# A GLA, short-convolution and SwiGLU block on one core: the queues' order is taken from the scheduler's more detailed timeline model

## The chip, the cores and the metric
The kernel runs on one core of a Trainium2 chip. The time is the device time of one execution in microseconds (us), and of several executions the median is taken. A core has five engines, each with its own queue of instructions that it works off in order: TensorE (PE in the profile, with PEld for its weight loads), VectorE (DVE), ScalarE (ACT), GpSimd (POOL) and SyncE (SP, which here only issues DMAs). Engines wait for one another by semaphores.

## The reference
One layer works on 512 latent tokens of width 2048 and 256 context tokens, all in fp32:

```python
hc = modulate(rmsnorm(ctx, norm1_g), sh1c, sc1c)       # context: only k, v and the forget gates are used
o_c, s_f, s_b = gla_bidir(qc, kc, vc, la_fc, la_bc, 0, 0)
hx = modulate(rmsnorm(x, norm1_g), sh1, sc1)
q, k, v, g, lf, lb, cb, cc, cx = split_proj(hx @ w_in)
o_x, _, _ = gla_bidir(q, k, v, la_f, la_b, s_f, s_b)   # 4 heads, forward and backward scan
o   = headwise_rmsnorm(o_x) * gla_g * silu(g)
mix = concat(o, cb * conv_grid(cc * cx, conv_w)) @ w_out
x1  = x + gt1 * mix
h2  = modulate(rmsnorm(x1, norm2_g), sh2, sc2)
out = rmsnorm(x1 + gt2 * ((silu(h2 @ wg) * (h2 @ wu)) @ wd), final_g)
```

The modulation rows (`sh1`, `sc1`, `gt1`, `sh2`, `sc2`, `gt2`) are `silu(c) @ w_mod + b_mod`, and `gla_bidir` is a chunked gated linear attention with data-dependent decay.

## The kernel before
**Products.** Every large product is fp32 made from three fp32r matmuls (`mm3`, L85 to L94): low part of one side by high of the other, high by low, high by high. A weight tile of 128x1024 is loaded by a DMA from SP into `raw` (L118, four buffers) or `ch` (L755, eight), ACT casts it to `whi` (L102), and DVE subtracts to give `wlo` (L103, three buffers each). A unit of the PE's work is the matmuls on one such pair.

**Stages, in the order of time.** (1) From 0 to about 390 us the k and v projections. The normalized input is scaled with modulation columns that the PE makes first from streamed tiles `big<-wsc` (`mod_cols`, L193 to L210, into `pm`); `hhi`, `hlo`, `hhl` and `chl` are its high and low parts. Squares of the input go from ACT to POOL, which adds them (L250). Constants `cid`, `cst` and `gates` are loaded at L265 to L267, and POOL makes eight masks `maskt` from `cst` (L270). (2) From about 390 to 850 us the attention. A function `weave` interleaves one head (`do_gla`) with units of projections (`do_q`, `do_g`, `do_conv`) as filling for the PE. A head has for each direction a chain: ACT makes `qe` and `ke` (L570, L572), DVE multiplies and copies them (L577 to L580; L578 is the last of `qe`) and `kk` (L586), the PE makes scores `psc`, DVE masks them (L596) and adds (L598), then four scan steps follow (`sm` on ACT L610, `pd` and `po` on the PE, `sn` on DVE L618), ACT normalizes (`on`, L633), the PE transposes the result into `pt` (L639) and DVE multiplies it by the gate (L641). Beside that, DVE makes the remaining modulation rows: `mod_some` (L373) multiplies 128 loaded tiles `raw<-wm` of 128x1024 with `cbc` and sums them; each must wait for its load, and its buffer is refilled only when it is done. (3) From about 850 to 1025 us the output projection, as a Strassen-like scheme with seven products (`seven`, steps "1", "5", "63", "7", "24"). The seven left operands are sums and differences of quarters, made by DVE and split into `a0h`, `a0l` to `a6h`, `a6l` (`prep_a`, L701 to L737); the right ones are made in place in `ch` (L782, L788, L793, L807). (4) To about 1125 us the second norm: ACT scales rows (L878), the PE transposes them (L888), ACT modulates (L893), and DVE makes operands again. (5) To about 1950 us the up and gate products of the FFN for eleven column blocks j, each with `seven`; `back` (L957) transposes the activations of the block before, `back_part` splits them and sends them to DRAM. (6) To about 2365 us the down product, and then the final norm (L1087) and the stores.

**What sets the order.** The program text does not fix the order in an engine's queue. The framework's scheduler, which runs when the context `tile.TileContext` closes, takes the instructions with their dependences and writes each engine's queue from a model of when things would be ready. The exception is SP from the start of stage (3) on (L690): there its order is that of the text. Buffers and data dependences are the same in any order.

## Time and profile before

| what | us |
|---|---|
| median of 3 runs (2388.7, 2388.78, 2394.04) | 2388.78 |
| profiled execution | 2393.07 |
| its span in the trace | 2391.3 |
| PE busy | 2252.2 |
| DVE busy | 1704.9 |
| ACT busy | 1030.8 |
| POOL busy | 136.3 |

The profiled execution is thus one of the longer ones, 4.3 us over the median. Its time is 1.8 us more than the span of its instructions. In the views each row has an engine, the line of the kernel, the operation with output and inputs by their names (buffer numbers left out), a count, busy time and, in square brackets or behind a bar, the idle time of that engine just before, with what ended it. PEclk is the granted clock of the PE, 1.00 being full speed; the mean over the execution was 0.973.

### The profile page before, as it was taken

The numbers are of one execution on the slowest core, as the hardware profiler recorded it, in microseconds if no ns is written. First come the engines' busy times: TensorE is split into PE (matmuls) and PEld (weight loads), VectorE is DVE, ScalarE is ACT, GpSimd is POOL, SyncE is SP. The second block draws the span as 40 slices with busy tenths as digits, with TensorE's granted clock in tenths as the row PEclk, the third lists the DMA queues.
The fourth block names the chain that finished last, engine by engine and source line by source line (L and its number), as shares of the span: only waits on it lengthen the run. The fifth ranks groups of instructions, "written<-read, shape, count | busy, mean of one in ns | idle before, by whom it ended". The sixth has DMA issues, their size and how long they took to land.

```text
span 2391.3 us, 27558 instructions
## 1 busy us (share of the span) xinstructions
PE 2252.2 (94%) x10184; PEld 1793.0 (75%) x10184; DVE 1704.9 (71%) x2088; ACT 1030.8 (43%) x1391; POOL 136.3 (6%) x186
## 2 busy tenths in 40 slices
PE   8999999888979969987999999999999999999996
PEld 4765666777868747765888888888888878888875
DVE  3555165665665577768887888788877867787798
ACT  3422055322232344475445554555454544443343
POOL 2422000000000000000000000000000000000001
PEclk9999999999989989998999999999999999999998
DMA  9773466665766244541446434544354494855734
GB/s 326 229 253 111 150 228 194 199 213 187 231 192 217 90 150 128 178 157 52 145 150 203 143 128 145 193 150 142 139 176 159 165 362 151 289 185 178 255 130 141
DMA packets 161619, 431.42 MB, mean 180 GB/s; under 512 B 17867, under 2 KB 38635, under 8 KB 161356
## 3 DMA queue, kind: packets, MB, share of 16 engines
q1 hardware_dynamic: 141612, 380.87, 48.1%
q0 software_dynamic: 8720, 28.58, 3.2%
q10 hardware_dynamic: 11152, 20.21, 2.3%
q8 instruction: 80, 1.31, 0.2%
q14 instruction: 55, 0.45, 0.1%
HBM read 380.82 MB, written 48.78 MB: 180 GB/s over the span
## 4 chain that ended last, share of the span: by engine, by line
issue 57%; POOL 2%; PE 2%; DVE 0%; POOLq 0%; ACT 0%
PE acc L90 2%; POOL opd L971 2%; POOL out L1088 0%; POOL xnd L927 0%; ACT whi L102 0%; DVE xn L925 0%; POOLq L971 0%; DVE wlo L103 0%; DVE u L924 0%; DVE g L922 0%; DVE u L827 0%; POOLq L1205 0%; POOLq L1088 0%; POOLq L927 0%
## 5 line engine op out<-in xcount | busy, mean ns | idle before, releaser
L102 ACT CAST whi<-ch 128x1024 fp32r<-128x1024 f32 x370 | 390.2, 1056 | 461.5 <-PE acc L90 380.4
L103 DVE TENSOR_TENSOR wlo<-ch,whi 128x1024 fp32r<-128x1024 f32 x370 | 450.5, 1224 | 153.8 <-ACT whi L102 153.0
L102 ACT CAST whi<-raw 128x1024 fp32r<-128x1024 f32 x244 | 256.4, 1053 | 405.7 <-PE acc L90 284.9
L103 DVE TENSOR_TENSOR wlo<-raw,whi 128x1024 fp32r<-128x1024 f32 x244 | 302.5, 1240 | 158.8 <-ACT whi L102 158.1
L373 DVE CUSTOM_DVE_ANT_0 raw<-raw,cbc 128x1024 f32<-128x1024 f32 x128 | 156.3, 1224 | 159.6 <-DMA raw<-wm 157.2
L90 PE MATMUL acc<-hhl,whi 128*128 128x512 f32 x640 | 200.0, 393 | 0.0
L90 PE MATMUL acc<-hhi,wlo 128*128 128x512 f32 x320 | 133.4, 418 | 9.1 <-DVE wlo L103 8.3
L90 PEld LDWEIGHTS acc<-hhl,whi 128*128 128x128 f32 x640 | 121.1, 190 | 27.3 <-issue 2.5
L90 PE MATMUL acc<-wlo,a0h 128*128 128x512 f32 x296 | 117.5, 397 | 25.1 <-DVE wlo L103 25.1
L90 PE MATMUL acc<-hhl,wlo 128*128 128x512 f32 x320 | 127.5, 398 | 0.0
L90 PE MATMUL acc<-hlo,whi 128*128 128x512 f32 x320 | 127.2, 397 | 0.2 <-DVE hlo L108 0.2
L90 PE MATMUL acc<-hhi,whi 128*128 128x512 f32 x320 | 126.8, 396 | 0.0
L90 PE MATMUL acc<-whi,a1l 128*128 128x512 f32 x296 | 117.3, 398 | 9.6 <-DVE a1l L103 8.0
L90 PE MATMUL acc<-wlo,a1h 128*128 128x512 f32 x296 | 117.2, 396 | 9.5 <-DVE wlo L103 9.5
L90 PE MATMUL acc<-whi,a6l 128*128 128x512 f32 x296 | 116.4, 395 | 8.8 <-ACT whi L102 7.5
L90 PE MATMUL acc<-whi,a2l 128*128 128x512 f32 x296 | 116.1, 395 | 6.4 <-ACT whi L102 6.4
L90 PE MATMUL acc<-wlo,a2h 128*128 128x512 f32 x296 | 118.0, 399 | 0.9 <-DVE wlo L103 0.9
L90 PE MATMUL acc<-whi,a2h 128*128 128x512 f32 x296 | 117.8, 398 | 0.0
L90 PE MATMUL acc<-wlo,a6h 128*128 128x512 f32 x296 | 116.6, 394 | 0.9 <-DVE wlo L103 0.9
L90 PE MATMUL acc<-whi,a1h 128*128 128x512 f32 x296 | 116.9, 395 | 0.0
L90 PE MATMUL acc<-wlo,a3h 128*128 128x512 f32 x296 | 115.6, 391 | 1.1 <-DVE wlo L103 1.1
L90 PE MATMUL acc<-wlo,a4h 128*128 128x512 f32 x296 | 115.4, 390 | 1.2 <-DVE wlo L103 1.2
(310 smaller groups left out, 4802.8 us busy)
## 6 DMA issues: line engine op xcount, KB each, us to landing
raw<-wm SPq DMA_DIRECT2D x128, 512.0 KB, 4.7
raw<-wu SPq DMA_DIRECT2D x92, 512.0 KB, 4.5
ch<-wu SPq DMA_DIRECT2D x88, 512.0 KB, 3.8
raw<-wc SPq DMA_DIRECT2D x48, 512.0 KB, 3.7
raw<-wd SPq DMA_DIRECT2D x47, 512.0 KB, 6.4
ch<-wd SPq DMA_DIRECT2D x44, 512.0 KB, 6.0
opd<-oh ACTq DMA_DIRECT2D x77, 256.0 KB, 3.1
opd<-ol POOLq DMA_DIRECT2D x77, 256.0 KB, 3.3
```

The source lines that it names most:

```text
L90: nc.tensor.matmul(o, l, r, start=start, stop=stop, skip_group_check=True)
L102: nc.scalar.copy(hi, src)
L103: (eng or nc.vector).tensor_tensor(lo, src, hi, op=ALU.subtract)
L373: nc.vector.tensor_tensor_reduce(out=w, in0=w, in1=cbc[:, hf * 1024 : hf * 1024 + 1024], scale=1.0, scalar=0.0, op0=ALU.mult, op1=ALU.add, ...
L971: nc.gpsimd.dma_start(opd[j][i, 1].rearrange("p k t -> p (k t)"), lo.bitcast(F32))
```

## The change
One argument is added where the kernel opens the context:

```diff
-    with tile.TileContext(nc) as tc:
+    with tile.TileContext(nc, schedule_with_timeline_sim=True) as tc:
         tile_hybrid_block(tc, *args)
```

The scheduler then orders the queues by a more detailed model of the timeline. The instructions are the same on all engines, but for one load of an activation table fewer on ACT. The queues of PE, DVE and ACT are changed in many places, by some rows each; SP and POOL mostly in the first 250 us.

On the PE, in the attention of head 0, the transposes `pt` of the normalized head output `on` stand among the units of a filling projection `acc_3451`. Before:

```order
L90 MATMUL acc_3451<-hhl_539,whi_3454 128x512 x2
L90 MATMUL acc_3451<-hhi_615,wlo_3503 128x512
L639 MATMUL pt_3488<-cidt_70,on_3429 128x128
L639 MATMUL pt_3494<-cidt_70,on_3429 128x128
L90 MATMUL acc_3451<-hlo_616,whi_3502 128x512
L639 MATMUL pt_3488<-cidt_70,on_3429 128x128
L639 MATMUL pt_3494<-cidt_70,on_3429 128x128
```

Now:

```order
L90 MATMUL acc_3451<-hhi_849,whi_3502 128x512
L90 MATMUL acc_3451<-hhl_890,wlo_3503 128x512
L639 MATMUL pt_3488<-cidt_70,on_3429 128x128 x2
L639 MATMUL pt_3494<-cidt_70,on_3429 128x128
L639 MATMUL pt_3488<-cidt_70,on_3429 128x128
L639 MATMUL pt_3494<-cidt_70,on_3429 128x128
```

They stand 15 matmuls of the projection later; in the other heads it is 12 to 18. The second `psc` group (second direction) of head 0 stands 5 matmuls later, that of head 2 seven.

On DVE, in the same stage at head 2, the chain of the two directions (`qe_4527` is the first, `qe_4588` the second) stands among modulation tiles (L373; the second L373 row of each pair reads the sum out). Before:

```order
L578 COPY qe_4527<-big_3249 128x4
L373 ISA raw_4806,modacc_73<-raw_4806,cbc_76 128x1024
L373 ISA modacc_73 128x1
L103 TENSOR_TENSOR wlo_4727<-raw_4724,whi_4726 128x1024
L575 COPY dc_4592<-qe_4588 128x4
L576 TENSOR_TENSOR dc_4592<-qe_4588 128x4
L579 TENSOR_TENSOR ke_4590<-ke_4590,big_1070 128x512
L577 TENSOR_TENSOR qe_4588<-qe_4588,big_3249 128x512
L580 COPY ke_4590<-big_1070 128x4
L586 TENSOR_TENSOR kk_4604<-kk_4604,big_4520 128x512
L578 COPY qe_4588<-big_3249 128x4
L373 ISA raw_4809,modacc_73<-raw_4809,cbc_76 128x1024
```

Now:

```order
L373 ISA raw_4806,modacc_73<-raw_4806,cbc_76 128x1024
L373 ISA modacc_73 128x1
L578 COPY qe_4527<-big_3249 128x4
L373 ISA raw_4809,modacc_73<-raw_4809,cbc_76 128x1024
L373 ISA modacc_73 128x1
L103 TENSOR_TENSOR wlo_4727<-raw_4724,whi_4726 128x1024
L575 COPY dc_4592<-qe_4588 128x4
L576 TENSOR_TENSOR dc_4592<-qe_4588 128x4
L579 TENSOR_TENSOR ke_4590<-ke_4590,big_1070 128x512
L586 TENSOR_TENSOR kk_4604<-kk_4604,big_4520 128x512
L577 TENSOR_TENSOR qe_4588<-qe_4588,big_3249 128x512
L580 COPY ke_4590<-big_1070 128x4
```

Directly behind that come `L373` on `raw_4848` and only then `L578 qe_4588`. One modulation tile has moved ahead of the first direction's last copy, and two more ahead of the second's. In heads 0, 1 and 3 one has moved ahead of the first and one more ahead of the second. The masks and scan steps that follow (L596, L618, L598) also have one or two more ahead of them.

On DVE at the output projection, `wlo_6119` and `wlo_6137` are the low halves of the third and fourth weight pair; the `a` rows are operands of the seven products. Before:

```order
L103 TENSOR_TENSOR a5l_6065<-big_4773,a5h_6064 128x256
L103 TENSOR_TENSOR a6l_6069<-big_4773,a6h_6068 128x256
L103 TENSOR_TENSOR wlo_6119<-ch_6116,whi_6118 128x1024
L103 TENSOR_TENSOR wlo_6137<-ch_6134,whi_6136 128x1024
L103 TENSOR_TENSOR wlo_6160<-ch_6078,whi_6159 128x1024
L782 TENSOR_TENSOR ch_6098<-ch_6177,ch_6098 128x1024
```

Now:

```order
L782 TENSOR_TENSOR ch_6078<-ch_6156,ch_6078 128x1024
L660 TENSOR_TENSOR big_5769<-big_5769,acc_5773 128x512
L782 TENSOR_TENSOR ch_6098<-ch_6177,ch_6098 128x1024
L103 TENSOR_TENSOR wlo_6119<-ch_6116,whi_6118 128x1024
L724 TENSOR_TENSOR s_5888<-big_3014,big_4966 128x256
L724 TENSOR_TENSOR s_5888<-big_3612,big_5187 128x256
```

`wlo_6119` has moved from the end of the operands to ahead of them, some 70 rows. `wlo_6137` follows 19 rows behind it and `wlo_6160` 22 rows behind that, with operand rows between.

Elsewhere: on ACT in stage (4), `whi_7313`, `whi_7332` and `whi_7399` have moved from behind the sixteen-fold L893 to ahead of the first L878; on the PE the transposes L888 now follow the units that use them. On DVE there `wlo_7784` stands 11 rows earlier. On SP a third tile of `wk` and `cid`, `cst` and `gates` (L265 to L267) now come ahead of the second group of `big<-wsc`, and `cbc` (L362) comes in the middle of stage (1); the eight masks L270 are the first work of POOL. In stage (5) the transposes L957 stand 20 to 30 rows earlier on the PE, and on DVE four rows L793 of a block, which read freshly loaded `raw` tiles, stand 3 to 12 rows earlier. At the very end two `wlo` rows of DVE stand 11 or 12 rows earlier.

## Prediction
> **What bounds the kernel now.** I read the page first, then the table of busy time by stage, then what the PE waits for.
>
> ```profile
> span 2391.3 us, 27558 instructions
> PE 2252.2 (94%) x10184; PEld 1793.0 (75%) x10184; DVE 1704.9 (71%) x2088; ACT 1030.8 (43%) x1391; POOL 136.3 (6%) x186
> ```
>
> The PE is idle for 2391.3 - 2252.2 = 139 us. An order can move only that, and the matmuls that ran at a low clock. Next is busy time by stretch: each engine with its count, then the granted clock, the DMA share and GB/s.
>
> ```profile
> 0.00:60.00 60.00, 49.25 (x303) 29.97 (x304) 22.31 (x31) 22.51 (x44) 16.32 (x19) 1.00 1.01 326
> 390.00:850.00 460.00, 417.34 (x1894) 346.36 (x1893) 271.37 (x450) 135.40 (x214) 0.00 (x0) 0.95 0.60 192
> 850.00:900.00 50.00, 24.38 (x98) 18.81 (x96) 43.16 (x95) 26.42 (x63) 0.00 (x0) 0.76 0.34 123
> 1020.00:1125.00 105.00, 81.28 (x351) 65.18 (x352) 83.68 (x111) 71.51 (x117) 2.18 (x4) 0.85 0.32 109
> 1125.00:1890.00 765.00, 764.63 (x3447) 632.95 (x3446) 626.31 (x632) 385.14 (x457) 35.31 (x65) 1.00 0.45 153
> ```
>
> The columns are PE, PEld, DVE, ACT and POOL. The FFN's first stage is full: 764.63 of 765 us, 764.63 / 3447 = 0.222 us a matmul. Idle time lies in four places: attention (460 - 417.34 = 42.7 us), the start of the output projection (25.6), the second norm (23.7) and the first 60 us (10.8). The view of the PE's waits says for whom.
>
> ```profile
> PE acc L90 <- DVE wlo L103: 47.0, 16, 22.2
> PE pt L639 <- ACT on L633: 22.0, 3, 8.7
> PE acc L90 <- ACT whi L102: 15.9, 7, 7.5
> PE psc L90 <- DVE qe L578: 13.5, 4, 3.9
> ```
>
> (Us in total, times, longest.) So a few long waits carry it, in which the PE's queue is stopped by one matmul, while DVE or ACT works off something else that stood ahead.
>
> **The change, part by part.** Each part is held against the profiled execution, 2393.07 us.
>
> *Attention, transposes.* Three transposes `pt` wait 22.0 us together. They now stand some 14 filling matmuls later, 14 x 0.222 = 3.1 us of work for each wait, none of which is as short as that: -9.4 us, if `on` isn't later.
>
> *Attention, chains.* DVE now has modulation tiles ahead of the chain, and these wait for loads. Head 2 in DVE's and SP's timelines:
>
> ```profile
> 659.31 0.17 DVE L578 COPY qe<-big 128x4 f32<-128x4 f32 x1
> 660.12 1.22 DVE L373 CUSTOM_DVE_ANT_0 raw<-raw,cbc 128x1024 f32<-128x1024 f32 x1 [0.65 <-DMA raw<-wm]
> 661.27 1.22 DVE L103 TENSOR_TENSOR wlo<-raw,whi 128x1024 fp32r<-128x1024 f32 x1
> 664.43 0.17 DVE L578 COPY qe<-big 128x4 f32<-128x4 f32 x1
> 664.50 1.22 DVE L373 CUSTOM_DVE_ANT_0 raw<-raw,cbc 128x1024 f32<-128x1024 f32 x1
> 666.98 1.23 DVE L373 CUSTOM_DVE_ANT_0 raw<-raw,cbc 128x1024 f32<-128x1024 f32 x1 [1.25 <-DMA raw<-wm]
> ```
>
> ```profile
> raw<-wm SPq DMA_DIRECT2D x128, 512.0 KB, 4.7
> ```
>
> The page's row gives 4.7 us from issue to landing. The first tile is now ahead of `qe_4527`, whose copy moves from 659.31 to 661.3, behind the wait. The second tile was ready long before 664.50; with it (1.15) and `wlo` (1.15) DVE is at 664.3 when the refill for the third tile can be issued, which in the old order was at 662.5, the end of that `wlo`; it landed there at 666.98, 4.5 later, so now at 668.8. The chain's own four rows take DVE to 666.3, then it stands until 668.8, does the tile (1.15), and copies `qe_4588` at 670.0 instead of 664.43: 5.6 later. The PE does seven matmuls meanwhile (1.6), so 4.0 is lost. The PE waits there already:
>
> ```profile
> 443.30 2.04 PE L90 MATMUL psc<-qe,ke 128*128 128x128 f32 x8 [3.06 <-DVE qe L578]
> ...
> 664.74 2.05 PE L90 MATMUL psc<-qe,ke 128*128 128x128 f32 x8 [3.08 <-DVE qe L578]
> ...
> 783.43 1.13 PE L90 MATMUL psc<-qe,ke 128*128 128x128 f32 x8 [3.25 <-ACT a0h L102]
> ```
>
> Heads 0 and 3 have the same waits at their second `psc`. There one tile is ahead of each direction. In head 0 the second tile landed only after the chain:
>
> ```profile
> 443.96 1.23 DVE L373 CUSTOM_DVE_ANT_0 raw<-raw,cbc 128x1024 f32<-128x1024 f32 x1 [0.81 <-DMA raw<-wm]
> ```
>
> With the chain behind its end at 445.2 (2.1 us, as in head 2 from the end of `wlo` at 662.5 to that of the copy at 664.6) `psc` comes at 447.3: 4.0 later, less five matmuls, 2.9. For head 3, where a tile (1.15) and some operand rows come ahead and nothing fills, I take 3.5; for head 1, without a wait now, 1.5 of the 2.3 that two tiles cost. Sum 4.0 + 2.9 + 3.5 + 1.5 = 11.9, and the attention comes to +2.5 us. Bounds: if those tiles cost nothing, -9.4 and the 2.7 of the filled `psc`, -12; if the scan steps, which also have tiles ahead, deliver `on` later by what the filling gave, +12. I take the middle, since the waits for loads stand in the rows.
>
> *Output projection.* One long wait on the PE, and what DVE did in it:
>
> ```profile
> 857.17 0.73 PE L90 MATMUL acc<-whi,a1l 128*128 128x512 f32 x2 [1.56 <-ACT whi L102]
> 880.07 0.80 PE L90 MATMUL acc<-wlo,a0h 128*128 128x512 f32 x1 [22.17 <-DVE wlo L103]
> 880.66 0.63 PE L90 MATMUL acc<-whi,a0h 128*128 128x512 f32 x1
> 881.09 0.63 PE L90 MATMUL acc<-whi,a0l 128*128 128x512 f32 x1
> ...
> 899.03 0.73 PE L90 MATMUL acc<-whi,a2l 128*128 128x512 f32 x2 [1.67 <-ACT whi L102]
> ```
>
> ```profile
> 857.32 1.10 DVE L726 TENSOR_TENSOR s<-s,big 128x256 f32<-128x256 f32 x3
> ...
> 878.75 3.53 DVE L103 TENSOR_TENSOR wlo<-ch,whi 128x1024 fp32r<-128x1024 f32 x3
> ```
>
> For 878.75 - 857.32 = 21.4 us DVE makes 64 operand rows, 0.335 each, and only then the `wlo`. Now `wlo_6119` comes first, but about 20 rows (6.7 us) stand between it and the next `wlo`, while a unit of 12 matmuls is 2.7 us of PE. The long wait becomes several, each some 4: row by row I get 5.4, 7.0, 3.0, 1.1 and 4.3, 20.8 us, against 1.56 + 22.17 + 1.67 = 25.4. That is -4.6, not -22: DVE was busy 43.16 of 50 us, so at most 6.8 can go without work moved ahead of 850. Bounds -7 and 0.
>
> After such a wait matmuls come 881.09 - 880.66 = 0.43 apart instead of 0.222. [...]
>
> *Second norm.* Two waits:
>
> ```profile
> 1031.22 7.37 ACT L893 ACTIVATE hbig<-pt,modv,gsc 128x256 f32<-128x256 f32 x16
> ```
>
> ```profile
> 1044.94 1.22 PE L90 MATMUL acc<-whi,a6l 128*128 128x512 f32 x2 [7.51 <-ACT whi L102]
> ...
> 1053.46 0.39 PE L90 MATMUL acc<-whi,a0l 128*128 128x512 f32 x1
> ...
> 1106.86 0.80 PE L90 MATMUL acc<-wlo,a1h 128*128 128x512 f32 x1 [8.07 <-DVE wlo L103]
> ```
>
> `whi_7313` stood behind L893 and the casts that follow it, and now comes before; the units run through. But then the PE transposes, and L893 (7.37) with a cast and a split must pass before `a0l`: I count a wait of about 9.6 there, and the matmul of 1053.46 at 1050.6. -3. `wlo_7784` is 11 rows (0.60 each) earlier on DVE, so 8.07 becomes 3.5 by my count; a new wait of 3.8 for `wlo_7843` follows, and with the earlier start about -4 stays. Bounds for both: -12 and 0.
>
> *Start.* `cid` (128 KB), `cst` (576), `gates` (132) and a `wk` tile (512) now come ahead of the second `wsc` group: 1.38 MB at the 326 GB/s of the first row, 4.2 us, with the DMA share at 1.01. The PE needs these tiles for its first modulation columns, and with 49.25 of 60 us busy it has some reserve later. I take +3; bounds 0, if SP's issues run ahead of need, and +6, if POOL's masks, which wait for `cst`, hold up its sums and ACT behind them as well.
>
> *FFN.* L793, L957 and the first matmuls of units move; the PE's 764.63 of 765 us covers them, as its next `whi` and `wlo` lie ready. 0, while the `raw` loads come in time. *Rest.* Two `wlo` at the very end and one small wait near 1020: -2.
>
> Sum: 2.5 - 4.6 - 7 + 3 - 2 = -8. That gives 2385 against the profiled execution. It lies 4.3 us above the median of 2388.78 (runs from 2388.7 to 2394.04), so I forecast 2381.
>
> **The rivals.** *Tiles cost nothing* (time 2366): the loads for L373 have landed when DVE comes to them, so the attention gives its -12: 2388.8 - 8 - 14.5. For it: the tile at 664.50 was taken without a wait; against it: [0.65] and [1.25] above are waits for loads, and a refill can't be issued before DVE frees the buffer. *Slower, by DVE's head-of-line waits* (time 2404): in every head the moved tiles hold `qe`, the masks and `sn`, `on` comes later by more than the filling, +12; the loads at the start cost 6; the output projection gives nothing and the norm half, -3. Together +15. It decides from the point where the heads lose more than about 5 us each. *The order counts for little* (2388): each wait of the PE only moves to the next due time, since what DVE and ACT must do in a stage is the same; for it speaks 43.16 of 50.
>
> **How the numbers follow.** Forecast .38, tiles free .24, slower .25, little .13. A measurement of this kernel can tell about 0.3%, 7.2 us, from no change: faster is below 2381.6, slower above 2396. The forecast's own range, 2373 to 2391, lies about half and half on both sides of 2381.6: .20 faster, .17 the same, .01 slower. Tiles free gives .24 faster. Slower gives .22, and .03 the same. Little gives .12 the same, .01 faster. Sum: faster .45, same .32, slower .23. The range that leaves out no more than 2 in 10 goes from below tiles free to the slower case: 2360 to 2404.
>
> **What would show it.** In the profile after: waits at `pt` L639 near 13 us in all instead of 22; waits of `psc` on L578 grown from 13.5 to over 20; no wait of 22.17 but some of 3 to 7 near 860 to 890; the first `a0l` matmul after the norm some 3 us earlier in its stage; a PE at 765 of 765 in the FFN. Waits of the PE inside the FFN, or `psc` waits that shrink, would prove it wrong.

## The result, and the profile after

The changed kernel takes 2481.05 us (median of 4 runs, 2480.32 to 2487.05), the kernel before 2391.41 us on the same chip (4 runs, 2388.7 to 2395.23). The ratio is 1.0384, with a 95% interval of 1.0369 to 1.0398: slower by some 90 us, where 8 us faster was forecast, and 77 us above the range. The profiled execution took 2487.05 us with a span of 2485.3, 94 us over the 2393.07 of before.

First the page's span and busy times.

```profile
span 2485.3 us, 27612 instructions
PE 2294.8 (92%) x10184; PEld 1808.1 (73%) x10184; DVE 1688.0 (68%) x2088; ACT 1025.7 (41%) x1390; POOL 134.9 (5%) x186
```

The same 10184 matmuls. Idle time has gone from 139 to 2485.3 - 2294.8 = 190.5 us, which is 51 of the 94; the other 43 are in busy time, 2294.8 against 2252.2. In the projection, below, 6.0 of the 8.1 us are longer steps from one matmul to the next behind waits, most of them 0.43 us instead of 0.222; for the other stages it isn't divided. Then busy time by stretch (PE, PEld, DVE, ACT, POOL, granted clock, DMA share, GB/s): the first 60 us, the attention's heads, the two FFN stages.

```profile
0.00:60.00 60.00, 46.29 (x292) 29.18 (x296) 18.15 (x28) 24.55 (x43) 17.61 (x27) 1.00 1.01 334
420.00:903.00 483.00, 421.29 (x1860) 346.38 (x1859) 264.36 (x440) 128.65 (x207) 0.00 (x0) 0.93 0.56 177
1180.00:1957.00 777.00, 766.43 (x3442) 632.86 (x3441) 621.45 (x630) 383.77 (x456) 35.14 (x65) 1.00 0.45 150
1957.00:2468.00 511.00, 483.23 (x2077) 390.98 (x2075) 384.79 (x401) 208.34 (x237) 9.46 (x18) 0.98 0.58 203
```

The FFN's first stage, full before at 764.63 of 765, now has 10.6 us without a matmul in 777. The second stage took 485 us before, with these counts:

```profile
1890.00:2375.00 485.00, 472.98 (x2071) 388.40 (x2070) 385.29 (x400) 207.80 (x236) 10.33 (x19) 0.99 0.61 214
```

And the PE's waits after (us in total, times, longest).

```profile
PE acc L90 <- DVE wlo L103: 58.1, 43, 4.8
PE psc L90 <- DVE qe L578: 37.2, 8, 9.8
PE acc L90 <- ACT whi L102: 24.3, 9, 8.0
PE pt L639 <- ACT on L633: 10.7, 3, 4.5
```

The one wait of 22.2 us is gone and the `pt` waits are halved, as meant; `wlo` now comes late 43 times where it was 16, and `psc` waits almost three times as long.

For the rest I use a lag. The same matmuls run in both kernels, so at each place where the first so many matmuls are the same set in both, the time by which all of them are done can be subtracted. The places are the end of the first loads' stretch, the start of the last value matmuls, the beginning of the heads, their end, the end of the projection, the middle of the FFN's first block, and the end of its up and of its down part (times in us in the span; the lags of the experiments stand in the same columns):

| kernel | 101 | 310 | 384 | 840 | 995 | 1132 | 1893 | 2362 |
|---|---|---|---|---|---|---|---|---|
| after | +5.1 | +11.5 | +23.9 | +54.6 | +59.7 | +55.1 | +68.3 | +93.2 |
| loads_back | +4.5 | +10.8 | +16.0 | +12.8 | +14.3 | +11.7 | +10.1 | +25.5 |
| mod_rows_back | +5.7 | +12.5 | +18.7 | +6.3 | +11.2 | +5.6 | +13.8 | +33.2 |
| ffn_rows_back | +5.9 | +12.5 | +24.5 | +50.4 | +51.6 | +48.5 | +46.9 | +65.0 |
| fifth_raw_buffer | +4.5 | +10.0 | +24.0 | +49.9 | +55.1 | +51.6 | +49.7 | +64.6 |
| raw_rows_back | +6.4 | +13.3 | +18.5 | +9.6 | +8.0 | +5.2 | +4.0 | +5.1 |
| raw_rows_and_loads_order | -2.0 | +2.8 | +8.0 | -1.0 | -1.1 | -5.3 | -6.5 | -4.0 |
| early_loads_alone | +0.3 | +0.0 | +10.6 | +18.9 | +21.4 | +23.6 | +40.0 | +49.6 |
| dve_queue_alone | +9.6 | +9.8 | +16.7 | +48.2 | +54.5 | +58.7 | +73.6 | +93.5 |
| dve_queue_back | +9.0 | +19.3 | +32.7 | +26.6 | +26.2 | +29.2 | +33.9 | +35.9 |
| dve_queue_and_loads_order | -1.6 | +11.6 | +25.5 | +18.5 | +18.2 | +20.7 | +29.4 | +30.8 |
| pe_order_back | +8.2 | +11.0 | +13.5 | +54.1 | +60.6 | +60.4 | +68.1 | +90.0 |
| spliced | +0.5 | +0.3 | -0.4 | -12.5 | -12.3 | -16.3 | -17.9 | -18.6 |

The loss comes from everywhere but the second norm: 5.1 at the start, 18.8 up to the heads, 30.7 in the heads, 5.1 in the projection, -4.6 in the norm, 13.2 and 24.9 in the FFN.

What happens there can be seen in one block of the FFN. DVE's timeline of before: L807 subtracts a freshly loaded `raw` tile, L103 makes the low half of a weight.

```profile
1345.57 1.23 DVE L807 TENSOR_TENSOR ch<-raw,ch 128x1024 f32<-128x1024 f32 x1 [0.73 <-DMA raw<-wu]
...
1350.17 1.23 DVE L103 TENSOR_TENSOR wlo<-raw,whi 128x1024 fp32r<-128x1024 f32 x1 [0.50 <-ACT whi L102]
1351.73 1.23 DVE L807 TENSOR_TENSOR ch<-raw,ch 128x1024 f32<-128x1024 f32 x1 [0.34 <-DMA raw<-wu]
1352.89 1.23 DVE L103 TENSOR_TENSOR wlo<-ch,whi 128x1024 fp32r<-128x1024 f32 x1
1355.23 1.23 DVE L807 TENSOR_TENSOR ch<-raw,ch 128x1024 f32<-128x1024 f32 x1 [1.12 <-DMA raw<-wu]
```

The same rows in the timeline of after:

```profile
1406.60 1.23 DVE L807 TENSOR_TENSOR ch<-raw,ch 128x1024 f32<-128x1024 f32 x1 [1.34 <-DMA raw<-wu]
...
1412.63 1.22 DVE L807 TENSOR_TENSOR ch<-raw,ch 128x1024 f32<-128x1024 f32 x1 [1.33 <-DMA raw<-wu]
1413.77 1.22 DVE L103 TENSOR_TENSOR wlo<-raw,whi 128x1024 fp32r<-128x1024 f32 x1
1414.91 1.22 DVE L103 TENSOR_TENSOR wlo<-ch,whi 128x1024 fp32r<-128x1024 f32 x1
1418.87 1.22 DVE L807 TENSOR_TENSOR ch<-raw,ch 128x1024 f32<-128x1024 f32 x1 [2.74 <-DMA raw<-wu]
...
1421.21 1.22 DVE L103 TENSOR_TENSOR wlo<-ch,whi 128x1024 fp32r<-128x1024 f32 x1
```

The middle L807 and the `wlo<-raw` beside it have changed places. That `wlo` is the last reader of its `raw` buffer, and SP issues the next load as soon as it ends, 1351.42 before and 1415.02 after:

```profile
1351.42 0.33 SPq L118 DMA_DIRECT2D raw<-wu  x1
```

```profile
1415.02 0.33 SPq L118 DMA_DIRECT2D raw<-wu  x1
```

The next L807 starts 3.81 and 3.85 us after that issue. So it is a loop: an L807 that waits holds the `wlo` behind it, the `wlo` holds the buffer, the buffer holds the load, and the load holds the next L807. A turn of it takes 1412.63 - 1406.60 = 6.0 and 1418.87 - 1412.63 = 6.2 us, while the PE needs 24 x 0.222 = 5.3 us for the two products of a unit; before, the same turns were 6.2 and 3.5. The turn ahead of these took 4.9 us after and 6.8 before, so a turn of over 5.3 alone doesn't hold up the PE: what differs is that the wait of the third L807 is handed on to the fourth. The `wlo` of 1421.21, which stands behind that one, then comes too late:

```profile
1422.48 0.50 PE L90 MATMUL acc<-wlo,a4h 128*128 128x512 f32 x1 [1.26 <-DVE wlo L103]
```

In the heads it is L373, the modulation row, that stands ahead. DVE in head 2 of after, and the PE's `psc` there:

```profile
696.54 1.23 DVE L373 CUSTOM_DVE_ANT_0 raw<-raw,cbc 128x1024 f32<-128x1024 f32 x1 [4.20 <-DMA raw<-wm]
...
701.32 0.68 DVE L577 TENSOR_TENSOR qe<-qe,big 128x512 f32<-128x512 f32 x1
701.93 0.16 DVE L580 COPY ke<-big 128x4 f32<-128x4 f32 x1
704.70 1.23 DVE L373 CUSTOM_DVE_ANT_0 raw<-raw,cbc 128x1024 f32<-128x1024 f32 x1 [2.61 <-DMA raw<-wm]
705.85 0.08 DVE L373 DVE_READ_ACCUMULATOR2_ANT modacc<- 128x1 f32 x1
705.85 0.17 DVE L578 COPY qe<-big 128x4 f32<-128x4 f32 x1
```

```profile
706.16 2.05 PE L90 MATMUL psc<-qe,ke 128*128 128x128 f32 x8 [9.78 <-DVE qe L578]
714.25 2.05 PE L90 MATMUL psc<-qe,ke 128*128 128x128 f32 x8 [3.37 <-DVE qe L578]
```

A copy of 0.17 us, the last row of the first direction's chain, whose others end at 702.1, stands behind a load for 3.8 us, and the PE behind it. Before, the first `psc` of head 2 waited less:

```profile
659.62 2.05 PE L90 MATMUL psc<-qe,ke 128*128 128x128 f32 x8 [3.47 <-DVE qe L578]
```

The waits of `psc` in the two traces, first and second direction of each head, in us:

| kernel | head 0 | head 1 | head 2 | head 3 |
|---|---|---|---|---|
| before | 3.91, 3.06 | none | 3.47, 3.08 | 0.05, 3.25 |
| after | 2.64, 3.30 | 5.99, 2.38 | 9.78, 3.37 | 8.01, 1.78 |

The growth is nearly all at the first directions of heads 1 to 3; head 0 lost nothing there. DVE's waits for loads say how much longer it stands in all, before and after:

```profile
DVE raw L373 <- DMA raw<-wm: 157.2, 82, 5.6
DVE ch L807 <- DMA raw<-wu: 23.6, 30, 2.7
```

```profile
DVE raw L373 <- DMA raw<-wm: 203.8, 85, 4.9
DVE ch L807 <- DMA raw<-wu: 51.9, 31, 3.9
```

There are hardly more waits; they are longer on the mean, 2.4 us instead of 1.9 for L373 and 1.7 instead of 0.8 for L807.

### The profile page after: what moved, and what is told of

It reads as the page before. It is cut to its first block, busy times and chain, and to the rows that moved or that the text cites. A ratio compares the mean times of both kernels' runs of the same rounds, so it can differ in the third digit from the quotient of the medians.

```text
span 2485.3 us, 27612 instructions
## 1 busy us (share of the span) xinstructions
PE 2294.8 (92%) x10184; PEld 1808.1 (73%) x10184; DVE 1688.0 (68%) x2088; ACT 1025.7 (41%) x1390; POOL 134.9 (5%) x186
## 4 chain that ended last, share of the span: by engine, by line
issue 60%; PE 14%; DMA 14%; DVE 7%; POOL 2%; ACT 2%; POOLq 0%; SPq 0%; DVEq 0%; ACTq 0%
DMA raw<-wm 12%; PE acc L90 11%; DVE wlo L103 2%; DVE raw L373 2%; PE pm L90 2%; POOL opd L971 2%; PE pl L90 1%; DMA raw<-wo 1%; DMA big<-wsc 1%; ACT whi L102 0%; DMA raw<-wq 0%; POOL out L1088 0%; DMA raw<-wk 0%; DMA raw<-wv 0%; PE pb L90 0%
## 5 line engine op out<-in xcount | busy, mean ns | idle before, releaser
L103 DVE TENSOR_TENSOR wlo<-ch,whi 128x1024 fp32r<-128x1024 f32 x370 | 450.1, 1220 | 141.1 <-ACT whi L102 139.9
L103 DVE TENSOR_TENSOR wlo<-raw,whi 128x1024 fp32r<-128x1024 f32 x244 | 299.9, 1230 | 177.3 <-ACT whi L102 177.0
L373 DVE CUSTOM_DVE_ANT_0 raw<-raw,cbc 128x1024 f32<-128x1024 f32 x128 | 156.4, 1224 | 204.3 <-DMA raw<-wm 203.8
L807 DVE TENSOR_TENSOR ch<-raw,ch 128x1024 f32<-128x1024 f32 x74 | 90.4, 1223 | 79.3 <-DMA raw<-wu 51.9
L90 PE MATMUL acc<-wlo,a1h 128*128 128x512 f32 x296 | 120.0, 405 | 14.3 <-DVE wlo L103 14.3
L90 PE MATMUL acc<-wlo,a4h 128*128 128x512 f32 x296 | 117.4, 396 | 12.2 <-DVE wlo L103 12.2
L90 PE MATMUL acc<-whi,a1l 128*128 128x512 f32 x296 | 107.9, 404 | 12.9 <-DVE a1l L103 9.6
L90 PE MATMUL acc<-whi,a2l 128*128 128x512 f32 x296 | 105.8, 398 | 14.7 <-ACT whi L102 14.7
L90 PE MATMUL acc<-whi,a0h 128*128 128x512 f32 x296 | 116.4, 393 | 0.0
```

What stands on the lines that cost most here:

```text
L90: nc.tensor.matmul(o, l, r, start=start, stop=stop, skip_group_check=True)
L103: (eng or nc.vector).tensor_tensor(lo, src, hi, op=ALU.subtract)
L373: nc.vector.tensor_tensor_reduce(out=w, in0=w, in1=cbc[:, hf * 1024 : hf * 1024 + 1024], scale=1.0, scalar=0.0, op0=ALU.mult, op1=ALU.add, ...
L807: tt(a[u], c, a[u], op=ALU.subtract)
```

## The experiments

The theory after the result (A): VectorE rows that read a fresh load stand too early in its queue and start this loop. The rivals: TensorE's own new order costs it (B), or the new order of VectorE's other rows does (C). All kernels but one keep the kernel's text and set the order with edges that say only "issue this behind that", with no wait of their own. Whatever isn't named is planned anew by the scheduler around them, so other rows move a little too. The edit, shortened (in the kernels the pairs are numbers in a packed text):

```diff
-    with tile.TileContext(nc) as tc:
+    with tile.TileContext(nc, schedule_with_timeline_sim=True) as tc:
         tile_hybrid_block(tc, *args)
+        rows = {i.name: i for i in nc.cur_bb.bb.instructions}
+        for ahead, behind in PAIRS:
+            tc.add_manual_dep(rows[behind], ahead, NO_SYNC, reason="queue order")
```

### The load rows held back

**loads_back**: PAIRS holds each of the 350 rows behind the row ahead of it in before's queue.

> The more detailed model stays on; the 350 VectorE rows that read a fresh load first (L373 of the modulation rows, L782, L788 and L807 of the products) are each only held behind the row that stands ahead of them in the order of before. Theory A (these rows came too early in VectorE's queue, wait there for their load, hold up the wlo and chain rows behind them, and so delay the next load): most of the 38 us of the FFN and of the 43 us between 310 and 840 us goes, 2400 to 2415 us. Rival B (TensorE's own order, with more changes between the fp32 groups and the split products): the order of TensorE is nearly that of after, so 2465 us or more. Rival C (the order of the other VectorE rows, the splits and the prepared operands): those stay where after has them, so 2465 us or more.

**mod_rows_back**: the 128 rows of L373 alone.

> As the run loads_back, but for the 128 rows of L373 alone, which stand between 310 and 840 us. Theory A: of 2481 us the 43 us lost in that stretch go in great part, 2435 to 2460 us, and the FFN stays 38 us longer than before's. Rivals B and C: 2475 us or more.

**ffn_rows_back**: the 222 rows of L782, L788 and L807 alone.

> As the run loads_back, but for the 222 rows of L782, L788 and L807 alone (output projection and FFN). Theory A: the FFN's 38 us go, 2440 to 2455 us, and the attention stays as in after; with mod_rows_back the two gains add up to that of loads_back within 10 us. Rivals B and C: 2475 us or more.

**pe_order_back**: PAIRS are the neighbours in before's queue of TensorE's 9642 matmuls instead.

> The more detailed model stays on; TensorE's 9642 matmuls are held in the order of before, all other queues are free. VectorE's load rows stay early. Theory A: only the extra changes of matmul kind between 112 and 310 us can go (up to 12 us), 2465 to 2485 us. Rival B: most of the 90 us goes, under 2420 us.

Measured, beside 2388.79 us of before: loads_back 2417.51 us (ratio 1.0121, 1.0104 to 1.0137), mod_rows_back 2432.43 (1.0181, 1.0166 to 1.0196), ffn_rows_back 2459.44 (1.0296, 1.028 to 1.0311), pe_order_back 2484.04 (1.04, 1.0384 to 1.0415). Against the 2481 of after, the two halves give back 49 and 22 us, together 70, and both in one 64: A holds and the halves add up within 10. B falls: TensorE in its old order loses as much as in the new one. C falls for the most part, as in loads_back VectorE's other rows stayed where the model puts them. loads_back ends 2.5 over its 2415, ffn_rows_back 4 over its 2455, mod_rows_back 3 under its 2435: the table shows the up part flat (+11.7 to +10.1), but the down part still losing 15.4 and 18.1.

### The fifth kind of row

In the down part of loads_back, L793 rows stood ahead of `wlo` rows; they read the same fresh load as L788. **raw_rows_back** adds the 74 rows of L793 to the PAIRS of loads_back.

> loads_back, and the 74 rows of L793 held too: they read the same fresh load as L788, and their result is only wanted a step later. In loads_back the FFN's down part still loses 16 us (13 of them in waits for wlo rows and one whi that stand behind such rows), the up part nothing. If the L793 rows are that, 16 us less, 2400 to 2406 us, with the 16 us lost before 400 us left. If the rest of the down part comes from other rows (the update of y at L1067, the copies on ScalarE), 2413 us or more.

Measured: 2398.76 us (ratio 1.0034, 1.002 to 1.0048; before 2391.23). The down part's loss is 1.1 us by the table. DVE's waits for loads in this run, whole span, and the busy time in the FFN's up part:

```profile
DVE raw L373 <- DMA raw<-wm: 145.9, 81, 5.0
DVE ch L807 <- DMA raw<-wu: 10.8, 10, 1.6
```

```profile
1129.50:1893.00 763.50, 763.12 (x3446) 632.55 (x3445) 621.62 (x631) 382.41 (x456) 35.31 (x65) 1.00 0.46 153
```

Both waits are now shorter than before's 157.2 and 23.6, and the PE is full again. With 424 rows held, 82 of the 90 us are gone; 18.5 us are still lost by 384 us, of which the heads and the norm win back most.

### The reverse, and the loop

**early_loads_alone**: the model off, PAIRS puts the row that stands behind each of the 350 in after behind it here.

```diff
     with tile.TileContext(nc) as tc:
         tile_hybrid_block(tc, *args)
+        rows = {i.name: i for i in nc.cur_bb.bb.instructions}
+        for ahead, behind in PAIRS:
+            tc.add_manual_dep(rows[behind], ahead, NO_SYNC, reason="queue order")
```

> The reverse: the model is off, and the same 350 rows (L373, L782, L788, L807) are held ahead of the VectorE row that stands behind them in after; nothing else is set. Theory A: these rows alone bring the loss, 2440 to 2470 us. Theory that it takes the rest of the new order too: within 10 us of before, 2399 us or less.

Measured: 2442.61 us (ratio 1.0213, 1.02 to 1.0227). The rows alone, in an order that is otherwise the old planner's, bring over half of the loss, in the heads as in both parts of the FFN.

**fifth_raw_buffer**: the model on, order free. Every fifth of these loads goes to a buffer of its own (the edit in part; 17 becomes 15 wherever tag e stands).

```diff
-        return fpool.tile([P, NB], F32, tag="e", name=name, bufs=17)
+        return fpool.tile([P, NB], F32, tag="e", name=name, bufs=15)
...
+    turn = [-1]
...
+        def load_raw6(src):
+            turn[0] += 1
+            if turn[0] % 5 < 4:
+                return load_raw(src)
+            r = fpool.tile([P, 1024], F32, tag="rx", name="raw", bufs=1)
+            nc.sync.dma_start(r, src)
+            return r
...
-                    d = load_raw(wsrc(3, u))
+                    d = load_raw6(wsrc(3, u))
...
-                    c = load_raw(wsrc(2, u))
+                    c = load_raw6(wsrc(2, u))
```

> The model is on and the load rows stay early, but the products of the projection and the FFN take their raw loads from five buffers instead of four (the tiles of tag e go from 17 to 15 to make room). The loop of theory A (a late wlo row frees its raw buffer late, so the load that VectorE waits for next is issued late) breaks in the FFN: most of the 38 us lost there goes, 2440 to 2460 us; the attention's loss stays. If the early rows cost only by standing in front, without the loop through the buffers, at most 10 us go: 2471 us or more.

Measured: 2459.14 us (ratio 1.029, 1.0268 to 1.0312). In 762 us of the FFN's up part the PE's only wait is 0.4 us. The order was planned anew with the fifth buffer, and in the blocks of the up part the rows are as early as in after or earlier: the third L807 of a block stands ahead of the third and fourth `wlo<-raw`, in after of the fourth alone, in before of neither. DVE's waits for the loads in that stretch, after and then here, where the line of L807 is L816:

```profile
DVE ch L807 <- DMA raw<-wu: 45.9, 27, 3.9
```

```profile
DVE ch L816 <- DMA raw<-wu: 13.0, 15, 1.6
```

The up part's 13 us are gone with the rows still early, so there the loop through the buffers is the cost, not the place in the queue by itself. In the down part 15 us stay, by the lag (+49.7 at its start, +64.6 at its end). In the heads no run tests the loop: what mod_rows_back shows there is that the early L373 rows cost, not by which path.

### What was lost ahead of the heads, and VectorE's whole queue

**raw_rows_and_loads_order**: raw_rows_back, and SP's first 170 loads in before's order.

> raw_rows_back, and the first 170 loads of SyncE's queue in the order of before (the more detailed model puts three constant tables and a wk load ahead of the wsc loads at the start, and wsh loads behind wv loads later). raw_rows_back is 6 us behind before at 89 us of the span and 17 to 18 us behind at 345 to 420 us, and wins 13 back later. If the order of the loads is what costs at the start, the pm waits on wsc go from 8.5 back to 5.4 us and 3 to 6 us of the time go: 2391 to 2396 us. If also the rest up to 345 us hangs on the loads, 2383 to 2388 us. If neither does, 2397 to 2400 us.

Measured: 2391.53 us (ratio 1.0003, 0.9994 to 1.0012; before 2391.2): 7 us gone, all of the loss up to 310 us but 2.8. The `pm` waits on `wsc` are 5.5 us in all, as its first case had them. At the start of after the PE stands at each of four `wsc` tiles, the first of them in this row; with the old order of the loads the PE's next wait after 12.72 us is the 0.68 in the second.

```profile
19.12 0.65 PE L90 MATMUL pm<-big,silsh 128*32 128x128 f32 x8 [2.49 <-DMA big<-wsc]
```

```profile
19.34 0.38 PE L90 MATMUL pc<-smt,tm 128*128 128x2 f32 x2 [0.68 <-ACT tm L209]
```

**dve_queue_alone**: the model off, PAIRS are VectorE's 1961 neighbours in after's queue. **dve_queue_back**: the model on, the neighbours in before's queue.

> The model off, VectorE's whole queue in the order of after, the other queues free. early_loads_alone came to 2443 us with the 350 load rows. If the rest of VectorE's new order (L793, the operands, the splits) brings the rest of the loss, 2465 to 2490 us. If the rest comes from the other queues, 2435 to 2455 us.

> The model on, VectorE's whole queue (1961 rows) in the order of before, the other queues free. Theory A, with what raw_rows_back left: the loss stands in VectorE's queue, 2390 to 2403 us (the start's loads stay as in after). If the other queues have a loss of their own that the load rows only cover, 2410 us or more.

Measured: dve_queue_alone 2486.74 us (ratio 1.0397, 1.0382 to 1.0411): VectorE's order alone brings a loss as large as after's. The PE stands little at `psc` there and more at `wlo` rows, so the same order of VectorE costs at other rows beside other queues. Over the whole span:

```profile
PE acc L90 <- DVE wlo L103: 89.9, 63, 6.2
PE psc L90 <- DVE qe L578: 5.9, 5, 2.1
```

Of the 89.9 us, 39.5 lie in the heads (400 to 895 us), where after has 12.2.

dve_queue_back 2435.91 (1.0184, 1.0169 to 1.02), 33 over its first case, so the second holds, a loss that comes with the other queues: its FFN is cured (+29.2 to +35.9), but it has lost 32.7 us by 384. **dve_queue_and_loads_order** takes SP's 170 loads back too.

> dve_queue_back came to 2436 us, 33 us over what theory A allows; its loss stands ahead of 430 us of the span (20 us by 305 us, 32 by 380 us), and from there to the end only some 4 us come in all. Here the first 170 loads of SyncE also go back to the order of before. If the order of the loads is the cause (VectorE's rows in the old order wait for data that now lands in another order), 2392 to 2408 us. If it gives only what it gave to raw_rows_back, 7 us, then 2426 to 2431 us, and TensorE's or ScalarE's new order against VectorE's old one is left for the rest.

Measured: 2424.07 us (ratio 1.0132, 1.0115 to 1.0149), 12 us less, nearer to the second case. What remains is a mixture that neither planner made: in dve_queue_back, and in dve_queue_and_loads_order too, VectorE's row L343 once stands 31.1 us for a `pc` that TensorE now makes later, where in before that row waited 7.5.

```profile
DVE silsh L343 <- PE pc L90: 33.1, 3, 31.1
```

That this wait is what costs there is only argued, and the 25.5 us that dve_queue_and_loads_order has lost by 384 aren't divided further.

### A version that beats both

**spliced**: all five queues laid down, the model off: before's order to 400 us, loads_back's to 733 us of its span, before's to 1015, loads_back's to 1918, then before's. Shortened as above:

```diff
     with tile.TileContext(nc) as tc:
         tile_hybrid_block(tc, *args)
+        rows = {i.name: i for i in nc.cur_bb.bb.instructions}
+        for queue in QUEUES:
+            for ahead, behind in zip(queue, queue[1:]):
+                tc.add_manual_dep(rows[behind], ahead, NO_SYNC, reason="queue order")
```

> A candidate to beat both, with every queue laid down: the order of before to 400 us, that of loads_back through the heads (there TensorE gained 9.1 us on before, the pt waits), before's through the projection, loads_back's through the second norm and the FFN's up part (5.3 us gained), before's through the down part. 2389 less 9.1 and 5.3, and some lost at the four seams: 2374 to 2383 us. If what loads_back gains in the heads rests on its being late there (loads are further ahead of a late TensorE), it comes to 2389 us or more.

Measured: 2378.53 us (6 runs; ratio 0.9941, 0.9926 to 0.9956; before 2391.23), faster than both. Its waits in the heads (400 to 840 us):

```profile
PE psc L90 <- DVE qe L578: 16.5, 6, 5.1
PE pt L639 <- ACT on L633: 5.2, 3, 4.0
```

The later transposes are the gain that the prediction saw: 22.0 us at `pt` have become 5.2, with `psc` near its old 13.5.

## Why the prediction was wrong, step by step

**What bounds the kernel.** Right as far as it goes, and misleading in one place: a PE that is busy 764.63 of 765 us shows that the loads came in time in that order, not that there was slack. The L807 rows waited 23.6 us for loads before, and the prediction read none of these rows.

**Heads, transposes**: forecast -9.4, measured 10.7 against 22.0, -11.3. Right.

**Heads, chains**: forecast +11.9, measured 37.2 against 13.5, +23.7, or +20.4 if before's second wait in head 3 is counted too. The prediction called that one the same wait, but its row puts the 3.25 us down to ACT's `a0h`. That a load ahead of the chain's last copy costs was right; the size was about half, and the place was wrong. The sum put the loss on the second `psc` of heads 0, 2 and 3 (2.9, 4.0, 3.5), and the table above has it at the first of heads 1, 2 and 3 (6.0, 6.3, 8.0). In head 2 the sum moved the first copy by 2.0 and charged nothing for it; that `psc` waits 9.78 us, since the loads ahead of it are themselves late (4.20 and 2.61 in the rows above), and the second 3.37 where it was 3.08. The step worked with landing times of before, moved by what stands ahead in one head; that the delay adds from tile to tile is the likely reason, argued and not tested. (A slip of the sum in head 2 counts little: from 661.3 the copy, a tile and `wlo` take DVE to about 663.7, not 664.3, so 4.0 should be 3.4.)

**Heads, what the sum left out**: of the 30.7 us that the heads lost, `psc` and `pt` make 9. Waits for `wlo` rows, 12.2 where before has 3.5, and 11 us more of busy time (424.3 against 413.3) weren't in it; the granted clock was 0.93 instead of 0.95.

**Before the heads**: not in the sum, which had +3 for the start alone; measured +5.1 there, with +18.8 behind it. The loads' order has a part in both (with it taken back, -2.0 instead of +6.4 at 101 us, and 10.0 instead of 12.1 from there to 384), and the early L373 rows begin here (early_loads_alone loses 10.6 between 310 and 384).

**Output projection**: forecast -4.6, measured +5.1. Its waits came out about as large as worked out, smaller and more of them, though the longest, 7.98 us, is for a cast of ACT (`whi`) that the sum didn't have; the matmuls between them didn't. Busy time of the stretch, before and then after:

```profile
838.00:995.40 157.40, 129.17 (x541) 103.93 (x540) 125.69 (x178) 71.57 (x119) 4.50 (x8) 0.90 0.46 148
```

```profile
893.00:1056.00 163.00, 137.23 (x543) 107.46 (x542) 125.38 (x178) 70.27 (x119) 4.48 (x8) 0.88 0.44 144
```

Idle time fell by (157.40 - 129.17) - (163.00 - 137.23) = 2.5 us, where 4.6 was forecast, and busy time rose by 8.1 for two matmuls more. After the waits of 4.81 and 3.29 us the matmuls come 0.43 apart, as they did after the one long wait of before. The whole stretch has 55 steps of over 0.33 us from one matmul to the next without a wait between, 11.6 us more than at 0.222 each; before it has 30, with 5.6 us. That is 6.0 of the 8.1. The first of the two waits:

```profile
927.26 0.80 PE L90 MATMUL acc<-wlo,a1h 128*128 128x512 f32 x1 [4.81 <-DVE wlo L103]
927.86 0.63 PE L90 MATMUL acc<-whi,a1h 128*128 128x512 f32 x1
928.28 0.63 PE L90 MATMUL acc<-whi,a1l 128*128 128x512 f32 x1
```

After has five such stretches of matmuls some 0.43 apart, behind waits of 1.62 to 7.98 us, where before has three, behind waits of 1.62 to 22.17. The prediction saw the 0.43 behind the longest of these, and its -4.6 has nothing for it. What slows the matmuls there no run tests.

**Second norm**: forecast -7, measured -4.6. Right in sign; the `whi` wait of 7.5 is gone and the `wlo` wait of 8.1 is 3.6, but one of 8.2 us for `rs_r` (L144) has come.

**FFN and rest**: forecast 0 and -2, measured +13.2 and +24.9. This is the step that failed most: the term for the FFN was put at 0 because the PE was full, and it cost 38.1 us. It carried its condition, "while the `raw` loads come in time", and counted L793, L957 and the PE's rows as moved. That L807, and L788 and L782 with it, had changed places with `wlo` rows was not read from the order, and the refill that such a `wlo` releases was not followed; L793 was read and thought covered, and holding its rows back as well was worth some 19 us (2417.51 to 2398.76). The down part, where most of the 38.1 lies, had no term but the -2 for its last rows; the 764.63 of 765 us is a row of the up part. "Waits of the PE inside the FFN" were named as the proof against the forecast, and came.

**The rivals.** *Slower, by DVE's head-of-line waits* came nearest, with 2404: a load ahead of `qe`, the heads as one place and its point of decision hold (30.7 us in four heads, 7.7 each, where 5 decided). Its price doesn't: it had `on` later by more than the filling, and the waits at `pt` fell to 10.7 us; and it had nothing for the FFN. *Tiles cost nothing* and *the order counts for little* are refuted by mod_rows_back and early_loads_alone.

## What to carry to other kernels

When a planner moves rows, look first for those that wait for a load, and follow what stands behind each on its engine to the row that frees the buffer of the next load: with four buffers, as here, a place earlier by one row handed the wait for one load on to the next, and DVE's waits at L807 grew from 23.6 to 51.9 us. A full engine in the profile of before is no cover for that: the FFN's up part, busy for 764.63 of 765 us, lost 13.2. A turn longer than the work per turn (6.2 against 5.3 us here) is a sign to look, no proof: before had turns of 6.8 and 6.2 us beside a full PE. A better order can be put together from two planners' orders, stage by stage, once the lag of each stage is known.

## What the runs showed of the hardware

Where one wait of 22.2 us became several, more busy time came than idle time went, as the rows of the projection show: 8.1 against 2.5 us. Putting TensorE back into its old order gained nothing (2484.04 against 2481.05 us). One more buffer for the loads of the FFN was worth as much in the up part as the better order: +51.6 at the start of it and +49.7 us at its end in fifth_raw_buffer, where after goes from +55.1 to +68.3.
